# Three 256-column matmuls as one of 256 and one of 512 columns in the one-stream feed-forward products of an exact-float32 network

## The chip, the cores and the metric

The program runs on one core of a Trainium2 chip. The metric is the time of one execution on the device in microseconds (us). Three runs of the kernel before took 2123.69, 2127.23 and 2135.45 us; the median is 2127.23 us.

## What is computed

Two transformer blocks of two layers each, on 256 tokens with 1024 features. Nearly all the arithmetic is matrix products with weights that are read once. Block one has four feed-forward layers around two attention mixers, block two has two mixing sublayers (on two streams of 256 tokens, latent and context) and a feed-forward layer behind each. The feed-forward layers have 2816 hidden features:

```python
def swiglu(x, w1, w3, w2):
    return (jax.nn.silu(x @ w1) * (x @ w3)) @ w2

h = h + 0.5 * swiglu(rmsnorm(h, g[0]), ffn_w1[layer, 0], ffn_w3[layer, 0], ffn_w2[layer, 0])
...
mod = split_cols((sc @ w_mod[l] + b_mod[l])[:, None, :], (D_MODEL,) * N_MOD)
x = layer_norm(ALPHA * x + g1 * y) * ln1_g[l] + ln1_b[l]
x = layer_norm(ALPHA * x + g2 * swiglu_2(modulate(x, sh2, sc2), w_ffn_in[l], w_ffn_out[l])) \
    * ln2_g[l] + ln2_b[l]
```

The context stream goes through layer 0 of block two and is only read as keys and values in layer 1.

## The kernel before

**Exact products.** float32 operands are split into two parts, hi and lo, in a matmul format (`FR`) of the array, with hi + lo equal to the number. A product w x is then three matmuls into one PSUM accumulator, w_hi x_hi, w_hi x_lo and w_lo x_hi; `mm3` (L317) issues them at L323, L324 and L325. The weight block of 128 by 128 is the stationary operand, so each of the three loads weights (rows PEld), and the tokens, 256 columns, stream past it.

**Weights.** All weight blocks are packed in the order of use in one array, in 540 chunks of eight blocks. `Weights.load` brings a chunk in by DMA (tile `wst`), `prepare` makes hi on ACT (L279, `whi`) and lo on VectorE (DVE; L280, `wlo`). Four split chunks are held (`NHL`), so a chunk is split up to four chunks ahead of its use, and a buffer is free when TensorE (PE) has read the chunk in it.

**Up and down.** A feed-forward layer has 22 hidden groups of 128 features. For each group `j` the up loop takes 16 weight blocks (8 over the features, w1 and w3 in turn; two chunks) by `slab_fm`, 48 matmuls into one PSUM bank, 256 columns for w1 and 256 for w3. There are four such banks (tag `mm`). In block one (`ffn1_layer`, L835) the bank is multiplied by 1/rms (L860, DVE, 512 columns, from PSUM to `w`), ACT takes silu of one half (L862), DVE multiplies by the other (L863), and `split` makes the operands of the next product, `ghi` on ACT (L329) and `glo` on DVE (L330). In block two (`up_gen`) silu (L1506) and product (L1507) read the bank itself. The down loop makes eight blocks of 128 output features, each of 22 triples, and adds a block to the residual (L794, L814, L1541).

**One stream and two.** Block one has one stream. In block two, layer 1's feed-forward and parts of layer 0's (six groups each of context and latent, and half of the down products) have one; the rest of layer 0 takes latent and context side by side, with 512 columns per matmul.

**Work beside the loops.** `step` (L332) runs one step of background generators at the end of each group. In three layers of block one `mod_gen` (L691) is one of them: it computes c @ w_mod, 1024 columns at a time, without the array, since it has two vectors only. For each of 16 row blocks it multiplies a loaded `mw` by one column and adds: for the first vector on DVE (L722; the first row block of eight on ACT), for the second on ACT (L725) and GpSimd (POOL; L726). In the second layer `later_gen` builds small tables on DVE as well.

**Order.** Every engine works its queue in order; the queues are laid out by a scheduler from the program's order and its own estimates. Buffers of named pools come free in turn: `w1` has four, `w2` two.

Of the kernel before, what the change touches and what calls it, by code (L numbers as in the profile page):

```python
# [8 lines left out]
FT = mybir.dt.float32  # L9
# [15 lines left out]
# ---------------------------------------------------------------- vector columns  # L25
# [8 lines left out]
# row vectors, broadcast to all partitions: sinks, (g_q, g_k) x2, g_sgu x2  # L34
# [3 lines left out]
# constant columns after the identity: causal, window, cos, sin  # L38
# [85 lines left out]
def _rows(w, groups):  # L124
    """[1024, 1024] by groups of 128-row blocks, each group output-block-major."""
# [4 lines left out]
def _pairs(n, g):  # L130
    """Column order that puts head i of the first group beside head i of the second."""
# [117 lines left out]
# ---------------------------------------------------------------- the kernel  # L249
class Weights:  # L250
    """Streams the packed weights: load, split into two exact float32r parts, hand out blocks."""
# [33 lines left out]
    def block(self, i, w=1):  # L285
        """w adjacent 128-column blocks from block i of the stream."""
# [3 lines left out]
        hi, lo = self.hl[h]  # L290
        c = (i % 8) * 128
        return hi[:, c:c + w * 128], lo[:, c:c + w * 128]
class Body:
# [6 lines left out]
    # ---- small helpers  # L300
# [16 lines left out]
    def mm3(self, ps, w, x, first, last, swap=False):  # L317
# [3 lines left out]
        if swap:  # L321
            (wh, wl), (xh, xl) = (xh, xl), (wh, wl)
# [1675 lines left out]
```

## Time and profile before

| | before |
|---|---|
| median of three runs | 2127.23 us |
| profiled execution, span | 2129.9 us |
| TensorE matmul busy | 2058.5 us, 97% |
| TensorE weight load busy (beside matmuls) | 1885.2 us, 89% |
| VectorE busy | 1509.3 us, 71% |
| ScalarE busy | 1095.1 us, 51% |
| GpSimd busy | 397.0 us, 19% |
| mean granted TensorE clock | 0.983 |

The span is the time from the first to the last instruction of the one execution that the profiler took. A matmul row's length contains its way through the array, so successive rows overlap, and the distance between two starts is what one costs in a stream. VectorE's rows overlap a little in the same way. An engine's busy time says nothing of what it waits for: that is read from the gaps between rows and from what ended them.

### The profile page before, as it was taken

What the parts mean: (1) busy time and instruction counts of PE and PEld (TensorE: products, weight loads), DVE (VectorE), ACT (ScalarE), POOL (GpSimd) and SP (SyncE); (2) the same over time, 40 slices, a digit from 0 to 9 for tenths busy, and PEclk for the clock granted to TensorE, in tenths of its full rate; (3) what the DMA queues carried; (4) which work ended last, traced back from release to release, by engine and by line L of the source; (5) the groups of instructions that cost most, each with busy time, mean ns of one, the idle gap of its engine ahead of it and who ended that gap; (6) DMA issues with size and microseconds to landing.
All of it is one profiled execution on the core that took longest, in us unless ns stands there. A gap on an engine that the chain in (4) does not pass through costs nothing. (4 is left out here: it accounts for less than half of the span.)

```text
span 2129.9 us, 39152 instructions
## 1 busy us (share of the span) xinstructions
PE 2058.5 (97%) x15451; PEld 1885.2 (89%) x15451; DVE 1509.3 (71%) x2646; ACT 1095.1 (51%) x1890; POOL 397.0 (19%) x283
## 2 busy tenths in 40 slices
PE   8999999899999999999999999999999999999997
PEld 8989989889999997999988878888788889779997
DVE  6797886987599566886775867667754468576554
ACT  5564576554566456554544645444432345555443
POOL 1232141321044010210510002213500013003002
PEclk9999999999999999999999988999999999999999
DMA  6775635866576552555541312475663353124553
GB/s 217 266 261 183 199 121 193 268 214 217 179 247 205 190 191 91 197 175 183 185 126 64 107 60 85 141 256 188 203 192 124 130 165 115 52 81 136 181 185 103
DMA packets 117113, 355.40 MB, mean 167 GB/s; under 512 B 21781, under 2 KB 27624, under 8 KB 116480
## 3 DMA queue, kind: packets, MB, share of 16 engines
q1 hardware_dynamic: 115472, 344.54, 49.5%
q10 hardware_dynamic: 1456, 8.36, 1.1%
q8 instruction: 121, 1.98, 0.4%
q14 instruction: 64, 0.52, 0.1%
HBM read 351.66 MB, written 8.90 MB: 169 GB/s over the span
## 5 line engine op out<-in xcount | busy, mean ns | idle before, releaser
L280 DVE TENSOR_TENSOR wlo<-wst,whi 128x1024 fp32r<-128x1024 f32 x540 | 712.1, 1319 | 346.7 <-ACT whi L279 341.2
L323 PE MATMUL mm<-HI,whi 128*128 128x256 f32 (+1 forms) x2944 | 868.6, 297 | 12.9 <-ACT whi L279 8.5
L325 PE MATMUL mm<-HI,wlo 128*128 128x256 f32 (+1 forms) x2944 | 865.6, 295 | 6.7 <-DVE wlo L280 6.7
L324 PE MATMUL mm<-LO,whi 128*128 128x256 f32 (+1 forms) x2944 | 868.5, 296 | 1.1 <-DVE LO L1411 1.1
L279 ACT ACTIVATE whi<-wst 128x1024 fp32r<-128x1024 f32 x540 | 570.0, 1056 | 554.8 <-PE mm L324 307.6
L323 PEld LDWEIGHTS mm<-HI,whi 128*128 128x128 f32 x2944 | 565.4, 193 | 40.5 <-issue 12.5
L324 PEld LDWEIGHTS mm<-LO,whi 128*128 128x128 f32 x2944 | 568.0, 193 | 25.4 <-issue 12.3
L325 PEld LDWEIGHTS mm<-HI,wlo 128*128 128x128 f32 x2944 | 568.0, 193 | 23.6 <-DVE wlo L280 7.8
L325 PE MATMUL mm<-ghi,wlo 128*128 128x256 f32 (+1 forms) x1000 | 288.0, 288 | 2.5 <-DVE wlo L280 2.5
L324 PE MATMUL mm<-glo,whi 128*128 128x256 f32 (+1 forms) x1000 | 287.4, 288 | 1.5 <-DVE glo L330 1.5
L323 PE MATMUL mm<-ghi,whi 128*128 128x256 f32 (+1 forms) x1000 | 286.8, 288 | 0.0
L726 POOL TENSOR_TENSOR macc<-macc,mp 128x1024 f32<-128x1024 f32 (+1 forms) x70 | 168.8, 2411 | 382.0 <-ACT mp L725 346.4
L325 PEld LDWEIGHTS mm<-ghi,wlo 128*128 128x128 f32 x1000 | 191.3, 191 | 8.1 <-issue 3.5
L324 PEld LDWEIGHTS mm<-glo,whi 128*128 128x128 f32 x1000 | 191.4, 191 | 4.4 <-DVE glo L330 2.1
L323 PEld LDWEIGHTS mm<-ghi,whi 128*128 128x128 f32 x1000 | 191.1, 191 | 2.5 <-issue 0.8
L722 DVE SCALAR_TENSOR_TENSOR macc<-mw,sc,macc 128x512 f32<-128x512 f32 (+1 forms) x126 | 161.9, 1285 | 31.7 <-DMA mw<-in_wmod 22.4
L324 PE MATMUL mm<-wlo,HI 128*128 128x256 f32 x352 | 101.2, 288 | 3.4 <-DVE wlo L280 3.4
L323 PE MATMUL mm<-whi,HI 128*128 128x256 f32 x352 | 101.8, 290 | 0.0
L325 PE MATMUL mm<-whi,LO 128*128 128x256 f32 x352 | 100.4, 286 | 0.0
L725 ACT ACTIVATE mp<-mw,sc 128x1024 f32<-128x1024 f32 (+1 forms) x70 | 67.6, 973 | 32.2 <-DMA mw<-in_wmod 24.4
L525 POOL TENSOR_TENSOR sacc<-sacc,w 128x256 f32<-128x256 f32 x36 | 34.5, 959 | 252.7 <-ACT w L521 251.6
L329 ACT ACTIVATE ghi<-w 128x256 fp32r<-128x256 f32 (+1 forms) x120 | 51.1, 426 | 55.0 <-DVE w L863 47.4
(416 smaller groups left out, 2496.9 us busy)
## 6 DMA issues: line engine op xcount, KB each, us to landing
wst<-in_wall SPq DMA_DIRECT2D x540, 512.0 KB
mw<-in_wmod SPq DMA_DIRECT2D x48, 512.0 KB
mw<-in_wmod SPq DMA_DIRECT2D x96, 256.0 KB
brep<-bvec ACTq DMA_DIRECT2D x16, 384.0 KB
nab<-rrep SPq DMA_DIRECT2D x24, 96.0 KB
bias<-brep SPq DMA_DIRECT2D x4, 512.0 KB
bias<-brep SPq DMA_DIRECT2D x8, 256.0 KB
rrep<-in_rpb ACTq DMA_DIRECT2D x4, 348.8 KB
```

Source lines behind the costliest of these rows:

```text
L279: self.marks.append(self.nc.scalar.activation(hi, src, AF.Copy))
L280: self.nc.vector.tensor_tensor(lo, src, hi.bitcast(FT), op=OP.subtract)
L323: nc.tensor.matmul(ps, wh, xh, start=first, stop=False, skip_group_check=True)
L324: nc.tensor.matmul(ps, wh, xl, start=False, stop=False, skip_group_check=True)
L325: nc.tensor.matmul(ps, wl, xh, start=False, stop=last, skip_group_check=True)
L329: self.marks = [self.nc.scalar.activation(hi, src, AF.Copy), self.nc.vector.tensor_tensor(lo, src, hi.bitcast(FT), op=OP.subtract)]
L525: nc.gpsimd.tensor_tensor(st["acc"], st["acc"], sq, op=OP.add)
L722: nc.vector.scalar_tensor_tensor(acc[:, i], w, s, acc[:, i], op0=OP.mult, op1=OP.add)
L725: nc.scalar.activation(t, w, AF.Copy, scale=s)
L726: nc.gpsimd.tensor_tensor(acc[:, i], acc[:, i], t, op=OP.add)
```

## The change

For a product with one stream, hi and lo of x are kept side by side in one tile (`HL`, `ghl`), and mm3 gets a whole bank: w_lo x_hi goes as 256 columns into its first half, then w_hi [x_hi | x_lo] as 512 columns into both. The first half then holds w_lo x_hi + w_hi x_hi and the second w_hi x_lo. The halves are added on the way out: in an up loop by `joined`, where ACT copies the second half to SBUF and DVE adds the first to it; in a down loop by two additions to the residual. An up group takes two banks. The multiplication by 1/rms reads the joined result from SBUF. Hi and lo of a weight chunk lie in one tile (`whl`). Products with two streams, the projections and the attention keep their three matmuls.

```diff
     def prepare(self):
...
-        hi = self.split.tile([128, 1024], FR, name="whi")
-        lo = self.split.tile([128, 1024], FR, name="wlo")
-        self.marks.append(self.nc.scalar.activation(hi, src, AF.Copy))
-        self.nc.vector.tensor_tensor(lo, src, hi.bitcast(FT), op=OP.subtract)
-        self.hl[i] = (hi, lo)
+        w = self.split.tile([128, 2, 1024], FR, name="whl")
+        self.marks.append(self.nc.scalar.activation(w[:, 0], src, AF.Copy))
+        self.nc.vector.tensor_tensor(w[:, 1], src, w[:, 0].bitcast(FT), op=OP.subtract)
+        self.hl[i] = w
...
     def mm3(self, ps, w, x, first, last, swap=False):
...
+        wh, wl = w[:2]
+        xh, xl = x[:2]
+        if len(ps.shape) == 2 and len(xh.shape) == 2 and ps.shape[1] == 2 * xh.shape[1]:
+            nc.tensor.matmul(ps[:, :S], wl, xh, start=first, stop=False, skip_group_check=True)
+            nc.tensor.matmul(ps.rearrange("p (h t) -> p h t", h=2), wh, x[2], start=False, stop=last,
+                             skip_group_check=True)
+            return
         nc.tensor.matmul(ps, wh, xh, start=first, stop=False, skip_group_check=True)
         nc.tensor.matmul(ps, wh, xl, start=False, stop=False, skip_group_check=True)
         nc.tensor.matmul(ps, wl, xh, start=False, stop=last, skip_group_check=True)

+    def joined(self, dst, ps):
+        c = self.w1()
+        self.nc.scalar.activation(c, ps[:, S:], AF.Copy)
+        self.nc.vector.tensor_tensor(dst, ps[:, :S], c, op=OP.add)
...
-        self.HI = self.actp.tile([128, 2, KB, S], FR, name="HI")
-        self.LO = self.actp.tile([128, 2, KB, S], FR, name="LO")
+        self.HL = self.actp.tile([128, 2, KB, 2, S], FR, name="HL")
...
+    def slab_wide(self, x):
+        pss = [self.ps("mm") for _ in range(2)]
+        for k in range(KB):
+            for c in range(2):
+                self.mm3(pss[c], self.W.block(self.wpos + 2 * k + c), self.at(x, k), k == 0, k == KB - 1)
+        self.wpos += 16
+        return pss
...
-                nc.vector.scalar_tensor_tensor(hm, ps, scale, hm, op0=OP.mult, op1=OP.add)
+                for c in (0, S):
+                    nc.vector.scalar_tensor_tensor(hm, ps[:, c:c + S], scale, hm, op0=OP.mult, op1=OP.add)
...
-            gh = gp.tile([128, FB, S], FR, name="ghi")
-            gl = gp.tile([128, FB, S], FR, name="glo")
+            g = gp.tile([128, FB, 2, S], FR, name="ghl")
             for j in range(FB):
-                ps, = self.slab_fm([st["hl"]])
+                pss = self.slab_wide(st["hl"])
...
                 t = self.w2()
-                nc.vector.tensor_tensor(t, ps, st["r"][:, None, :].to_broadcast([128, 2, S]), op=OP.mult)
+                for c in range(2):
+                    self.joined(t[:, c], pss[c])
+                nc.vector.tensor_tensor(t, t, st["r"][:, None, :].to_broadcast([128, 2, S]), op=OP.mult)
...
             for m in range(KB):
-                ps = self.ps("mm")[:, :S]
+                ps = self.ps("mm")
                 for k in range(FB):
-                    self.mm3(ps, self.W.block(self.wpos + k), (gh[:, k], gl[:, k]), k == 0, k == FB - 1)
+                    self.mm3(ps, self.W.block(self.wpos + k), parts(g[:, k]), k == 0, k == FB - 1)
...
     def up_gen(self, js, streams, g, j0):
...
-                ps, = self.slab_fm([self.hl(1 - i)])
+                pss = self.slab_wide(self.hl(1 - i))
+                t = self.w2()
+                for c in range(2):
+                    self.joined(t[:, c], pss[c])
                 sl = self.w1()
-                a, b = ps[:, 0], ps[:, 1]
+                a, b = t[:, 0], t[:, 1]
...
     def down_gen(self, streams, g, evict, nk=FB // 2):
...
+                if len(streams) == 1:
+                    self.mm3(ps, w, parts(g(k, streams[0])), k == 0, k == nk - 1)
+                    continue
```

Two places in the queues show what moves. The first is TensorE's queue in an up loop of block one, before, two blocks of weights:

```order
L323 MATMUL mm<-HI,whi 128x256
L324 MATMUL mm<-LO,whi 128x256
L325 MATMUL mm<-HI,wlo 128x256
L323 MATMUL mm<-HI,whi 128x256
L324 MATMUL mm<-LO,whi 128x256
L325 MATMUL mm<-HI,wlo 128x256
```

and after the change, four blocks of weights of such a loop, the 512-column matmul first or second by where the cut falls:

```order
L332 MATMUL mm<-HL,whl 128x512
L331 MATMUL mm<-HL,whl 128x256
L332 MATMUL mm<-HL,whl 128x512
L331 MATMUL mm<-HL,whl 128x256
L332 MATMUL mm<-HL,whl 128x512
L331 MATMUL mm<-HL,whl 128x256
L332 MATMUL mm<-HL,whl 128x512
```

Three matmuls per block have become two, with the same columns in sum. The second place is VectorE's queue in the third layer's up loop, one group and the start of the next, before (`w` are the buffers of one group, L860 reads the bank, `wlo` are weight splits, L722 is the modulation multiply):

```order
L722 SCALAR_TENSOR_TENSOR macc<-mw,sc,macc 128x1024
L860 TENSOR_TENSOR w_7312<-mm,rstd 128x512
L280 TENSOR_TENSOR wlo<-wst,whi 128x1024
L863 TENSOR_TENSOR w_7314<-w_7314,w_7312 128x256
L280 TENSOR_TENSOR wlo<-wst,whi 128x1024
L330 TENSOR_TENSOR glo<-w_7314,ghi 128x256
L722 SCALAR_TENSOR_TENSOR macc<-mw,sc,macc 128x1024
```

and after the change (L343 is the addition in `joined`, L895 the multiply by 1/rms, L279 the weight split, L898 the product, L353 the low part of the next operand, L754 the modulation multiply):

```order
L754 SCALAR_TENSOR_TENSOR macc<-mw,sc,macc 128x1024
L279 TENSOR_TENSOR whl<-wst,whl 128x1024
L898 TENSOR_TENSOR w_6195<-w_6195,w_6187 128x256
L343 TENSOR_TENSOR w_6250<-mm,w_6251 128x256
L343 TENSOR_TENSOR w_6250<-mm,w_6254 128x256
L279 TENSOR_TENSOR whl<-wst,whl 128x1024
L353 TENSOR_TENSOR ghl<-w_6195,ghl 128x256
L754 SCALAR_TENSOR_TENSOR macc<-mw,sc,macc 128x1024
L895 TENSOR_TENSOR w_6250<-w_6250,rstd 128x512
L279 TENSOR_TENSOR whl<-wst,whl 128x1024
L898 TENSOR_TENSOR w_6258<-w_6258,w_6250 128x256
```

Between two L754 stand two additions more, and the additions of a group come ahead of the low part of the group before. ACT's queue at the same place, after the change (L897 silu, L342 the copies in `joined`, L278 the high part of the weights, L352 of the operand, L757 the second vector's multiply):

```order
L897 ACTIVATE w_6195<-w_6187 128x256
L342 ACTIVATE w_6251<-mm 128x256
L342 ACTIVATE w_6254<-mm 128x256
L278 ACTIVATE whl<-wst 128x1024
L352 ACTIVATE ghl<-w_6195 128x256
L757 ACTIVATE mp<-mw,sc 128x1024
L278 ACTIVATE whl<-wst 128x1024
```

The two copies stand between one group's silu and its high part; before, only a weight split stood there.

## Rows read from the trace of the kernel before

**Rows 1.** The page's busy times: us, share of the span, instructions.

```profile
PE 2058.5 (97%) x15451; PEld 1885.2 (89%) x15451; DVE 1509.3 (71%) x2646; ACT 1095.1 (51%) x1890; POOL 397.0 (19%) x283
```

**Rows 2.** All waits: who waited for whom, us in total, times, longest.

```profile
ACT whi L279 <- PE mm L324: 307.6, 183, 4.5
```

**Rows 3.** Timeline of PE, one stream: start us, us, engine, line, operation.

```profile
1979.75 0.28 PE L323 MATMUL mm<-HI,whi 128*128 128x256 f32 x1
...
1983.95 0.28 PE L325 MATMUL mm<-HI,wlo 128*128 128x256 f32 x1
```

**Rows 4.** Timeline of PE, two streams side by side.

```profile
1649.81 0.39 PE L323 MATMUL mm<-HI,whi 128*128 128x512 f32 x1
...
1654.80 0.39 PE L324 MATMUL mm<-LO,whi 128*128 128x512 f32 x1
```

**Rows 5.** Busy us in four up loops: window, length, PE, PEld, DVE, ACT, POOL.

```profile
83.00:158.00 75.00, 69.83 (x552) 67.13 (x551) 70.53 (x69) 43.65 (x58) 30.16 (x11) 0.98 0.79 267
...
362.00:507.00 145.00, 131.67 (x1035) 126.53 (x1034) 124.93 (x171) 76.84 (x104) 36.40 (x14) 0.95 0.72 238
...
575.00:705.00 130.00, 126.47 (x1029) 122.10 (x1028) 117.66 (x126) 78.36 (x106) 44.49 (x14) 1.00 0.67 218
...
1935.00:2058.00 123.00, 123.00 (x1028) 123.00 (x1027) 68.11 (x88) 58.76 (x89) 0.00 (x0) 1.00 0.57 188
```

**Rows 6.** Timeline of DVE, one step in the third layer's up loop.

```profile
603.98 1.27 DVE L722 SCALAR_TENSOR_TENSOR macc<-mw,sc,macc 128x1024 f32<-128x1024 f32 x1
605.18 0.68 DVE L860 TENSOR_TENSOR w<-mm,rstd 128x512 f32<-128x512 f32 x1
605.78 2.83 DVE L280 TENSOR_TENSOR wlo<-wst,whi 128x1024 fp32r<-128x1024 f32 x1
608.54 0.41 DVE L863 TENSOR_TENSOR w<-w,w 128x256 f32<-128x256 f32 x1
608.87 1.21 DVE L280 TENSOR_TENSOR wlo<-wst,whi 128x1024 fp32r<-128x1024 f32 x1
610.01 0.41 DVE L330 TENSOR_TENSOR glo<-w,ghi 128x256 fp32r<-128x256 f32 x1
610.34 1.27 DVE L722 SCALAR_TENSOR_TENSOR macc<-mw,sc,macc 128x1024 f32<-128x1024 f32 x1
```

**Rows 7.** Timeline of POOL, the same step.

```profile
604.22 3.31 POOL L726 TENSOR_TENSOR macc<-macc,mp 128x1024 f32<-128x1024 f32 x1 [3.06 <-ACT mp L725]
```

**Rows 8.** Timeline of DVE, one step in the first layer's up loop.

```profile
104.30 0.68 DVE L860 TENSOR_TENSOR w<-mm,rstd 128x512 f32<-128x512 f32 x1
...
105.23 3.43 DVE L722 SCALAR_TENSOR_TENSOR macc<-mw,sc,macc 128x1024 f32<-128x1024 f32 x1
...
111.19 0.68 DVE L860 TENSOR_TENSOR w<-mm,rstd 128x512 f32<-128x512 f32 x1
```

**Rows 9.** Timeline of DVE, end of the first layer's up loop.

```profile
155.37 0.68 DVE L860 TENSOR_TENSOR w<-mm,rstd 128x512 f32<-128x512 f32 x1
...
160.52 4.62 DVE L722 SCALAR_TENSOR_TENSOR macc<-mw,sc,macc 128x1024 f32<-128x1024 f32 x2
...
168.74 3.09 DVE L722 SCALAR_TENSOR_TENSOR macc<-mw,sc,macc 128x1024 f32<-128x1024 f32 x1
```

**Rows 10.** Groups by line and form: count, busy us, mean ns, idle before.

```profile
L279 ACT ACTIVATE whi<-wst 128x1024 fp32r<-128x1024 f32 x540 | 570.0, 1056 | 554.8 <-PE mm L324 307.6 <-issue 155.0 <-DMA wst<-in_wall 54.1
...
L722 DVE SCALAR_TENSOR_TENSOR macc<-mw,sc,macc 128x1024 f32<-128x1024 f32 x42 | 83.1, 1979 | 0.0
...
L1507 DVE TENSOR_TENSOR w<-w,mm 128x256 f32<-128x256 f32 x34 | 14.1, 414 | 0.0
...
L1506 ACT ACTIVATE w<-mm 128x256 f32<-128x256 f32 x34 | 12.4, 366 | 0.0
```

**Rows 11.** Timeline of DVE, two 512-column multiplies in the fourth layer.

```profile
961.98 0.69 DVE L1236 TENSOR_TENSOR ex<-ex,rstd 128x512 f32<-128x512 f32 x1
962.58 0.69 DVE L860 TENSOR_TENSOR w<-mm,rstd 128x512 f32<-128x512 f32 x1
```

More of the change, by code (lines that the diff above doesn't have):

```diff
@@ L676, in out_pairs @@
             for k in range(KB):
-                self.mm3(ps, self.W.block(self.wpos + k), (x[0][:, k], x[1][:, k]), k == 0, k == KB - 1)
+                self.mm3(ps, self.W.block(self.wpos + k), self.at(x, k), k == 0, k == KB - 1)
             self.wpos += KB
@@ L1035, in even_mixer @@
                 for k in range(2):
-                    self.mm3(dst, W.block(base + 4 * k + m), (ch[:, k], cl[:, k]), m != 1 and k == 0, k == 1)
+                    self.mm3(dst, W.block(base + 4 * k + m), self.at(chl, k), m != 1 and k == 0, k == 1)
             self.fm_evict(qidx[:, :2], ps.rearrange("p (c t) -> p c t", c=2), r2)
@@ L1242, in pre_norm_gen @@
         nc = self.nc
[L1243 removed]
+        hi, lo = self.hl(1 - i)[:2]
         mu, r = stat.finish()
@@ L1540, in f @@
                 R = self.R[i]
-                nc.vector.scalar_tensor_tensor(R[:, m], ps, self.mod(l, i, 5, m), R[:, m], op0=OP.mult, op1=OP.add)
+                for c in range(0, ps.shape[1], S):
+                    nc.vector.scalar_tensor_tensor(R[:, m], ps[:, c:c + S], self.mod(l, i, 5, m), R[:, m],
+                                                   op0=OP.mult, op1=OP.add)
                 if feed:
@@ L1549, in ffn2_layer @@
             if l == 1:
-                gh, gl = [lambda k, i, t=gp.tile([128, FB, S], FR, name=n): t[:, k] for n in ("ghi", "glo")]
-                self.weave((self.up_gen(range(FB), [0], gh, gl, 0), FB), (self.rests[0], 11))
-                self.finish(self.down_gen([0], gh, gl, evict(True), FB))
+                t = gp.tile([128, FB, 2, S], FR, name="ghl")
+                g = lambda k, i: t[:, k]
+                self.weave((self.up_gen(range(FB), [0], g, 0), FB), (self.rests[0], 11))
+                self.finish(self.down_gen([0], g, evict(True), FB))
                 self.final_norm(stats[0])
@@ L1556, in ffn2_layer, with g @@
             H = FB // 2
-            def store(n, early):
-                one = gp.tile([128, JSEP, S], FR, name=n + "x")
-                two = gp.tile([128, H - JSEP, 2, S], FR, name=n)
-                def f(k, i):
-                    if k >= JSEP:
-                        return two[:, k - JSEP].rearrange("p i t -> p (i t)") if i is None else two[:, k - JSEP, 1 - i]
-                    return None if i is None else early[k] if i else one[:, k]
-                return f
-            gh, gl = [store(n, e) for n, e in zip(("ghi", "glo"), self.early)]
-            both = [0, 1]
-            self.weave((self.up_gen(range(JSEP), [0], gh, gl, 0), JSEP), (self.rests[0], JSEP))
-            self.finish(self.up_gen(range(JSEP, H), both, gh, gl, 0))
-            self.finish(self.down_gen(both, gh, gl, evict(False)))
-            self.finish(self.up_gen(range(H, FB), both, gh, gl, H))
-            self.finish(self.down_gen([0], gh, gl, evict(True)))
+            one = gp.tile([128, JSEP, 2, S], FR, name="ghlx")
+            two = gp.tile([128, H - JSEP, 2, 2, S], FR, name="ghl")
+            def g(k, i):
+                if k >= JSEP:
+                    x = two[:, k - JSEP]
+                    return x.rearrange("p h i t -> p h (i t)") if i is None else x[:, :, 1 - i]
+                return None if i is None else self.early[k] if i else one[:, k]
+            both = [0, 1]
+            self.weave((self.up_gen(range(JSEP), [0], g, 0), JSEP), (self.rests[0], JSEP))
+            self.finish(self.up_gen(range(JSEP, H), both, g, 0))
+            self.finish(self.down_gen(both, g, evict(False)))
+            self.finish(self.up_gen(range(H, FB), both, g, H))
+            self.finish(self.down_gen([0], g, evict(True)))
             self.drain()
```

80 lines of the change are left out of this document (41 added, 39 removed).

## The prediction

> **What bounds the kernel now.** I read the page's busy times first, then the waits, then TensorE's timeline to get its pace, then the busy times by stage. TensorE is busy for 97% of the 2129.9 us span [rows 1], so the program as a whole is paced by its matmuls, and the reader should see that ACT's long waits are waits for TensorE to give weight buffers back [rows 2]. The pace itself: in an up loop with nothing else going on, 35 starts take 1983.95 - 1979.75 = 4.20 us, 120.0 ns for each 256-column matmul [rows 3]. With two streams side by side, 22 starts take 4.99 us, 226.8 ns for 512 columns [rows 4]. So 256 more columns cost 106.8 ns, and every matmul with its own weight load has about 13.2 ns on top.
>
> The share of 97% is a mean, though. Of the four layers of block one, three run the modulation work (L691 to L726) beside their up loop. By stage, VectorE is busy 70.5 of 75, 124.9 of 145 and 117.7 of 130 us there, against 68.1 of 123 in the last layer of block two [rows 5]. One step of the third layer shows who sets the time: from 603.98 to 610.34 seven VectorE rows stand without a gap, 6.36 us, while the group's 48 matmuls need 48 x 0.120 = 5.76 [rows 6]. In that step a weight split takes 2.83 us where the next one takes 1.21, because GpSimd's add runs from 604.22 for 3.31 us [rows 7]; L860, which reads PSUM, runs through that same add in its normal 0.68. In the first layer it is L722 that is held, 3.43 instead of 1.27, and a step is 111.19 - 104.30 = 6.89 us [rows 8]. So these steps are VectorE's, all others TensorE's.
>
> **The change part by part.** *Matmuls.* Wherever one stream is multiplied (mm3's new branch) three matmuls of 256 columns become one of 256 and one of 512. By the program's order 14,842 matmuls become 11,834: 3,008 triples are rewritten, 122 up groups of 16 (88 in block one, 34 in block two) and 1,056 in down loops. A triple is 3 x 120.0 = 360.0 ns, a pair 120.0 + 226.8 = 346.8, so 13.2 ns a triple and 39.7 us if TensorE paced all of them. The columns are the same; only one weight load with its fixed part goes.
>
> The Trainium skill weighs in here. "TensorE: Matmul & The Clock Gate", section Back-to-back issue gap, gives N/2.4 + 2.5 ns for an isolated matmul, by which a triple would fall only by an estimated 2.5 ns; my rows have 13.2 at both widths, and the measurement decides.
>
> *Way out of an up group.* Each group gains two ACT copies of 256 columns from PSUM (366 ns each, L1506 [rows 10]) and two VectorE adds of 256 columns with one operand in PSUM (414 ns, L1507 [rows 10]). Successive VectorE rows start 0.07 to 0.08 us before the one ahead has ended (608.54 + 0.41 against 608.87 [rows 6]), so an add costs 0.335 and the pair 0.67 us. The multiply by rstd stays at 512 columns but reads SBUF twice; L1236 of that kind takes 0.69 like L860 and 0.60 to the next start [rows 11]: no difference where GpSimd is still. ACT has 43.7 to 78.4 us of work in these loops of 75 to 145 [rows 5], so its 0.58 us per group fits; if it did not, the price would be 0.58 x 122 = 71 us, the upper end.
>
> In a step with L722, VectorE without collision needs two splits at 1.135, L860 0.60, two short rows at 0.335 and L722 at 1.20: 4.74 us. With the adds it is 5.41. GpSimd's collision comes on top: 1.62 in the third layer (2.83 - 1.21), 2.16 in the first (3.43 - 1.27). 5.41 + 2.16 = 7.57 us, and TensorE's new group is 48/3 x 0.3468 = 5.55. So the steps that VectorE set before, it sets by more, and TensorE's saving there buys nothing. L722 appears 42 times [rows 10], three of them behind the first layer's last group [rows 9]: 39 steps. In the second layer small table operations crowd the same loop (171 VectorE instructions against 126 [rows 5]); I count 4 more groups. 43 x 0.67 = +28.8 us.
>
> *A collision that gets longer.* In the third layer L860 shielded 0.54 us of the add (2.16 - 1.62), since with an operand in PSUM it ran beside GpSimd [rows 6, 7]. Its successor reads SBUF alone, and in the new order it, or a split, follows L722 directly. If it is held like the splits, 14 steps lose 0.54: +7.6 us; if not, 0. I take 7.6, since the rows that are held here (L280, L722) read SBUF only. The Trainium skill has the same rule, in "GPSIMD Engine Reference", section 8. Key points: GpSimd shares its SBUF interfaces with VectorE, in contention with instructions that have two SBUF inputs. The trace agrees (2.83 against 1.21 for the split, 0.68 unchanged for L860).
>
> *The rest.* The remaining 79 up groups and 1,056 down triples are TensorE's: (79 x 16 + 1,056) x 13.2 ns = 2,320 x 13.2 = -30.6 us. Down evictions double (one more short row of 0.34 us each, by the starts in [rows 6]), beside 22 pairs of 7.6 us per block: hidden, and +0.34 only at the last of each layer. The first group now needs the low half of its weights first, some tenths of a us. Together +1. With two banks a group the four PSUM banks hold two groups instead of four: TensorE may run one group ahead, not three. Where it sets the pace a bank has 5.55 us to be read, against 0.37 + 0.67 of work behind at most one whi on ACT (1.06, L279 [rows 10]) and one split on VectorE: free. If that cover went, it is the second rival.
>
> Sum: -30.6 + 28.8 + 7.6 + 1 = +6.8, so 2129.9 + 6.8 = 2136.7 on the profiled run's clock, whose span is 2.7 above the median of the timed runs (2127.23). I forecast 2134 us. Between the ends: no added VectorE cost (-30.6) would give 2097; all of ACT's copies exposed as well, +71, 2205.
>
> **Rivals.**
> *A. VectorE's idle takes the adds.* The three loops leave VectorE idle for 4.5, 20.1 and 12.3 us [rows 5], 36.9 in sum, about what I add (36.4). If half of it can be used, the time is 2134 - 18 = 2116; if all, 2098. For it: the second layer's 20 us. Against it: the steps of rows 6 have no idle at all, and what is idle lies in steps without L722.
> *B. The new handoff stalls a full queue; slower than before.* In the new order the adds of group j stand in VectorE's queue ahead of the split and glo of the group before, and each waits for an ACT copy that stands behind silu and, at worst, whi (1.06). Behind the waiting add stand wlo, glo, L722 and all that needs them: ghi's partner, GpSimd's add, TensorE's weights. Each of the 43 steps could lose up to 1.06 us: 2134 + 43 x 0.5 = 2156 at half, 2180 at worst. It decides if VectorE idles over 0.25 us per step ahead of the adds. Against it: TensorE, needing 5.55 of 7.57 us, has each group ready some 2 us early.
> *C. The saving does not come.* No row shows a 256- and a 512-column matmul in turn; if the pair keeps the fixed 13.2 ns of the third load, the 30.6 us are gone: 2165, and 2149 if half of it stays. Against it: the 13.2 stands on both widths alike. By the 2.5 ns of the Trainium skill's "TensorE: Matmul & The Clock Gate", Back-to-back issue gap, it would be an estimated 2159.
> *D. Nothing happens* because mm3's branch isn't taken: excluded by TensorE's queue after the change, where 3,008 of the 512-column form stand.
>
> **How the numbers follow.** About 0.5% is what a measurement of this kernel can tell from no change, so 2117 to 2138 counts as the same. Forecast 0.52, own range 2118 to 2148: same 0.41, slower 0.11. A 0.18: faster 0.15, same 0.03. B 0.26: slower 0.24, same 0.02. C 0.04: slower. Together faster 0.15, same 0.46, slower 0.39. The range for 8 in 10 cuts the far halves of A and B: 2110 to 2164.
>
> **What would show it.** Pairs starting every 0.347 us in up loops of the last layer, whose step falls from 5.76 to 5.55. Steps with the modulation multiply at 7.0 to 7.6 us, VectorE full, TensorE waiting on wlo or on banks; the multiply by rstd held to over 2 us beside GpSimd in the third layer. TensorE's busy share falls in the three loops and its clock may dip below 1.00 more often than the 0.95 and 0.98 of rows 5; if it stays low for whole loops, all is slower than my range. If steps stay near 6.4 us, A was right; if VectorE idles ahead of its adds, B.

## The result, and the profile after

The change made the kernel slower: 2188.91 us median of 4 runs (2177.30 to 2190.33) against 2125.46 (2116.03 to 2135.45), a ratio of 1.0292 with a 95% interval of 1.0260 to 1.0324, some 63 us. The forecast was 2134, within a range that ended at 2164: a loss of 7 us became one of 63. The profiled run took 2190.33 us with a span of 2188.5, 58.6 above the profiled span of before.

The page's busy line of the changed kernel, as [rows 1]:

```profile
PE 2060.7 (94%) x12443; PEld 1739.5 (79%) x12443; DVE 1637.7 (75%) x2946; ACT 1168.1 (53%) x2134; POOL 386.8 (18%) x283
```

TensorE starts fewer matmuls, is busy for as long as in [rows 1], and so for a smaller share of a longer program. What it waits for is new. From the waits of the changed kernel (who waits for whom, us in total, times, longest):

```profile
PE mm L331 <- DVE w L343: 59.0, 35, 3.6
DVE w L343 <- ACT w L342: 19.7, 32, 3.5
```

L331 is the first matmul of a pair; it waits for the add L343, that is, for the two banks of the up group two before its own. Among the longer waits of before there was none of the kind.

Where the 58.6 us arise is read by stage. An up loop is measured from the first to the last start of its multiply by rstd (L860, now L895; in block two from product to product), 22 groups each:

| stage, us | before | after | difference | forecast |
|---|---|---|---|---|
| first three up loops | 129.9 + 143.5 + 128.0 | 146.3 + 150.9 + 147.5 | +43.3 | +31.5 |
| fourth up loop | 117.7 | 130.8 | +13.1 | -4.6 |
| block two, first product to first two-stream product | 100.9 | 107.1 | +6.2 | -2.5 |
| last up loop | 118.4 | 115.2 | -3.2 | -4.6 |
| all else (down loops, mixers, ends) | | | -0.8 | -13.0 |
| sum | | | +58.6 | +6.8 |

Each stage is read from one execution of a kernel. The first three up loops, which the runs e1, e10 and e11 below leave as before, took 399.8, 399.7 and 392.9 us there and 401.4 us in the kernel before, so a few us of a stage can't be told from nothing.

The same stretches as busy times, as in [rows 5] (window, length, PE, PEld, DVE, ACT, POOL, granted clock, DMA share, GB/s); they are the up loops of the first, second, third and fourth layer and of the last layer of block two:

```profile
25.00:172.00 147.00, 130.81 (x717) 108.99 (x716) 129.12 (x162) 86.84 (x143) 29.46 (x11) 0.99 0.71 236
381.00:532.00 151.00, 129.92 (x683) 108.84 (x682) 139.10 (x213) 89.57 (x146) 36.61 (x14) 0.92 0.68 224
600.00:748.00 148.00, 129.93 (x695) 109.24 (x695) 138.61 (x163) 89.04 (x148) 37.69 (x14) 0.94 0.60 193
908.00:1040.00 132.00, 122.08 (x671) 104.56 (x670) 106.61 (x182) 78.88 (x148) 15.23 (x14) 0.97 0.52 167
1998.00:2114.00 116.00, 115.27 (x654) 99.84 (x653) 86.50 (x127) 72.11 (x131) 12.10 (x7) 1.00 0.59 190
```

Three cases stand here. In the third layer VectorE is nearly full (138.6 of 148). In the last row nothing is full but TensorE, and the loop got shorter. The fourth row is neither: VectorE has 25 us to spare, and yet TensorE stands still for 10 us and its clock is at 0.97.

**A step of the third layer.** VectorE, from one product to the next, then GpSimd's row (start, us, engine, line), to set beside [rows 6, 7]:

```profile
643.25 0.41 DVE L898 TENSOR_TENSOR w<-w,w 128x256 f32<-128x256 f32 x1
643.59 0.74 DVE L343 TENSOR_TENSOR w<-mm,w 128x256 f32<-128x256 f32 x2
644.25 1.21 DVE L279 TENSOR_TENSOR whl<-wst,whl 128x1024 fp32r<-128x1024 f32 x1
645.38 0.68 DVE L895 TENSOR_TENSOR w<-w,rstd 128x512 f32<-128x512 f32 x1
645.99 2.62 DVE L353 TENSOR_TENSOR ghl<-w,ghl 128x256 fp32r<-128x256 f32 x1
648.53 1.27 DVE L754 SCALAR_TENSOR_TENSOR macc<-mw,sc,macc 128x1024 f32<-128x1024 f32 x1
649.73 1.21 DVE L279 TENSOR_TENSOR whl<-wst,whl 128x1024 fp32r<-128x1024 f32 x1
650.86 0.41 DVE L898 TENSOR_TENSOR w<-w,w 128x256 f32<-128x256 f32 x1
```

```profile
645.68 2.65 POOL L758 TENSOR_TENSOR macc<-macc,mp 128x1024 f32<-128x1024 f32 x1 [5.57 <-ACT mp L757]
```

No gap, and 650.86 - 643.25 = 7.61 us, the 7.57 of the forecast. The two adds take 0.66 (643.59 to 644.25). The row that is held beside GpSimd is the low half of the product (L353), 2.62 us in place of 0.41, and not the multiply L895. L895 had started 0.30 us ahead of GpSimd's add (645.38 against 645.68); L353 is the first row that starts behind it. An L895 that started behind such an add, in the first layer, was held in its turn (VectorE's row, then GpSimd's):

```profile
79.82 2.90 DVE L895 TENSOR_TENSOR w<-w,rstd 128x512 f32<-128x512 f32 x1
```

```profile
79.59 2.59 POOL L758 TENSOR_TENSOR macc<-macc,mp 128x1024 f32<-128x1024 f32 x1 [56.92 <-ACT mp L757]
```

In the groups by line and form this row's mean went from 451 ns before (L330) to 845 after, over 110 rows each (count, busy us, mean ns, idle before):

```profile
L330 DVE TENSOR_TENSOR glo<-w,ghi 128x256 fp32r<-128x256 f32 x110 | 49.6, 451 | 0.5 <-ACT ghi L329 0.5
```

```profile
L353 DVE TENSOR_TENSOR ghl<-w,ghl 128x256 fp32r<-128x256 f32 x110 | 92.9, 845 | 5.1 <-ACT ghl L352 4.8
```

**A stop in the fourth layer.** There is no modulation work there, but the entry of the context stream runs in the background (L1476 to L1485, L1224, L1480). ACT's rows, VectorE's and TensorE's around 920 us:

```profile
917.04 1.06 ACT L278 ACTIVATE whl<-wst 128x1024 fp32r<-128x1024 f32 x1 [1.26 <-PE mm L332]
919.92 1.06 ACT L278 ACTIVATE whl<-wst 128x1024 fp32r<-128x1024 f32 x1 [1.82 <-PE mm L332]
920.88 0.37 ACT L1482 ACTIVATE w<-st 128x256 f32<-128x256 f32 x1
922.60 0.42 ACT L1224 ACTIVATE w<-ex 128x256 f32<-128x256 f32 x1 [1.35 <-DVE ex L1485]
922.93 0.64 ACT L342 ACTIVATE w<-mm 128x256 f32<-128x256 f32 x2
```

```profile
921.01 1.23 DVE L279 TENSOR_TENSOR whl<-wst,whl 128x1024 fp32r<-128x1024 f32 x1 [1.65 <-ACT whl L278]
922.15 0.42 DVE L1485 TENSOR_TENSOR ex<-cx,w 128x256 f32<-128x256 f32 x1
923.32 0.76 DVE L343 TENSOR_TENSOR w<-mm,w 128x256 f32<-128x256 f32 x2 [0.75 <-ACT w L342]
```

```profile
919.44 0.40 PE L332 MATMUL mm<-HL,whl 128*128 128x512 f32 x1
919.67 0.59 PE L1480 MATMUL st<-sacc,ones 128*128 128x256 f32 x2
923.89 0.55 PE L331 MATMUL mm<-HL,whl 128*128 128x256 f32 x1 [3.63 <-DVE w L343]
924.24 0.63 PE L332 MATMUL mm<-HL,whl 128*128 128x512 f32 x1
924.67 0.41 PE L331 MATMUL mm<-HL,whl 128*128 128x256 f32 x1
924.88 0.63 PE L332 MATMUL mm<-HL,whl 128*128 128x512 f32 x1
```

Read it from the end. TensorE's fifth group waits until 923.89 for the banks of the third, whose matmuls ended about 914.0. The adds that empty them wait for ACT's copies at 922.93. Those stand in ACT's queue behind a weight split that waits for TensorE (until 919.92, when the fourth group is over), behind L1482, which reads a sum that TensorE makes behind that fourth group, and behind L1224, which waits for VectorE's L1485, itself behind a weight split. So third and fourth group have to be over before the third is read, and with two groups of banks nothing is left for TensorE to do.

The price is more than the wait. After it pairs start every 0.64 us until about 929.1. The granted clock, third column from the end, of the wait, of the eight pairs after it, and of the time behind those:

```profile
919.90:923.80 3.90, 0.37 (x2) 0.00 (x0) 2.04 (x4) 2.29 (x5) 0.00 (x0) 0.83 0.59 163
923.90:929.10 5.20, 5.20 (x16) 4.48 (x17) 2.88 (x7) 1.91 (x5) 1.42 (x2) 0.50 0.22 81
929.40:934.00 4.60, 4.60 (x28) 4.03 (x28) 2.56 (x4) 2.85 (x4) 0.00 (x0) 1.00 0.00 0
```

0.50 is the lower of the two levels, 1.2 GHz, at which a pair's 768 columns take 0.64 us. Eight pairs lose 8 x (0.64 - 0.35) = 2.3 us there, on top of 3.6 us of wait. The busy share hides this part, since a slow TensorE is a busy one.

### The profile page after: what moved, and what is told of

Read it like the earlier page. It is cut to its first block, busy times and chain, and to the rows that moved or that the text cites. A ratio compares the mean times of both kernels' runs of the same rounds, so it can differ in the third digit from the quotient of the medians.

```text
span 2188.5 us, 33896 instructions
## 1 busy us (share of the span) xinstructions
PE 2060.7 (94%) x12443; PEld 1739.5 (79%) x12443; DVE 1637.7 (75%) x2946; ACT 1168.1 (53%) x2134; POOL 386.8 (18%) x283
## 4 chain that ended last, share of the span: by engine, by line
PE 71%; DVE 17%; issue 6%; ACT 4%; DMA 3%; POOL 0%; ACTq 0%; SPq 0%; DVEq 0%; POOLq 0%
PE mm L332 23%; PE mm L331 12%; PE mm L335 8%; PE mm L336 8%; PE mm L337 8%; DVE whl L279 5%; DVE macc L754 3%; PE sc L1635 3%; DVE ghl L353 2%; ACT whl L278 2%; PE half L1676 2%; DMA mw<-in_wmod 1%; DMA wst<-in_wall 1%; DVE w L343 1%; PE tp L1664 1%
## 5 line engine op out<-in xcount | busy, mean ns | idle before, releaser
L279 DVE TENSOR_TENSOR whl<-wst,whl 128x1024 fp32r<-128x1024 f32 x540 | 682.6, 1266 | 269.3 <-ACT whl L278 267.7
L278 ACT ACTIVATE whl<-wst 128x1024 fp32r<-128x1024 f32 x540 | 569.9, 1057 | 476.1 <-PE mm L332 212.2
L332 PE MATMUL mm<-HL,whl 128*128 128x512 f32 x1952 | 709.4, 408 | 3.5 <-DVE HL L1446 3.3
L331 PE MATMUL mm<-HL,whl 128*128 128x256 f32 x1952 | 557.5, 290 | 76.2 <-DVE w L343 57.9
L331 PEld LDWEIGHTS mm<-HL,whl 128*128 128x128 f32 x1952 | 381.9, 196 | 98.3 <-issue 56.2
L332 PEld LDWEIGHTS mm<-HL,whl 128*128 128x128 f32 x1952 | 376.7, 195 | 92.0 <-issue 4.1
L332 PE MATMUL mm<-ghl,whl 128*128 128x512 f32 x960 | 341.1, 399 | 0.9 <-DVE ghl L353 0.9
L335 PE MATMUL mm<-HL,whl 128*128 128x256 f32 (+1 forms) x992 | 309.3, 318 | 5.2 <-DVE qk_t L1699 3.1
L336 PE MATMUL mm<-HL,whl 128*128 128x256 f32 (+1 forms) x992 | 311.2, 315 | 0.0
L337 PE MATMUL mm<-HL,whl 128*128 128x256 f32 (+1 forms) x992 | 310.2, 315 | 0.0
L331 PE MATMUL mm<-ghl,whl 128*128 128x256 f32 x960 | 270.1, 283 | 7.9 <-DVE whl L279 6.8
L332 PEld LDWEIGHTS mm<-ghl,whl 128*128 128x128 f32 x960 | 180.9, 189 | 45.7 <-issue 1.7
L335 PEld LDWEIGHTS mm<-HL,whl 128*128 128x128 f32 x992 | 187.7, 192 | 26.0 <-issue 10.7
L336 PEld LDWEIGHTS mm<-HL,whl 128*128 128x128 f32 x992 | 190.4, 192 | 17.3 <-issue 6.2
L337 PEld LDWEIGHTS mm<-HL,whl 128*128 128x128 f32 x992 | 190.0, 192 | 14.1 <-issue 2.7
L331 PEld LDWEIGHTS mm<-ghl,whl 128*128 128x128 f32 x960 | 182.2, 190 | 10.9 <-DVE whl L279 7.3
L754 DVE SCALAR_TENSOR_TENSOR macc<-mw,sc,macc 128x512 f32<-128x512 f32 (+1 forms) x126 | 164.4, 1305 | 27.4 <-DMA mw<-in_wmod 18.0
L343 DVE TENSOR_TENSOR w<-mm,w 128x256 f32<-128x256 f32 x244 | 92.5, 416 | 20.4 <-ACT w L342 19.7
L336 PE MATMUL mm<-whl,HL 128*128 128x256 f32 x352 | 101.8, 290 | 3.6 <-DVE whl L279 3.6
L353 DVE TENSOR_TENSOR ghl<-w,ghl 128x256 fp32r<-128x256 f32 (+1 forms) x120 | 100.9, 840 | 5.8 <-ACT ghl L352 5.5
L342 ACT ACTIVATE w<-mm 128x256 f32<-128x256 f32 x244 | 82.1, 375 | 38.6 <-PE mm L332 33.9
```

The costliest lines, as they stand in the source:

```text
L278: self.marks.append(self.nc.scalar.activation(w[:, 0], src, AF.Copy))
L279: self.nc.vector.tensor_tensor(w[:, 1], src, w[:, 0].bitcast(FT), op=OP.subtract)
L331: nc.tensor.matmul(ps[:, :S], wl, xh, start=first, stop=False, skip_group_check=True)
L332: nc.tensor.matmul(ps.rearrange("p (h t) -> p h t", h=2), wh, x[2], start=False, stop=last, skip_group_check=True)
L335: nc.tensor.matmul(ps, wh, xh, start=first, stop=False, skip_group_check=True)
L336: nc.tensor.matmul(ps, wh, xl, start=False, stop=False, skip_group_check=True)
```

## The experiments

Three explanations stood against each other: VectorE has too much work (adds); the way from ACT's copy to VectorE's add stalls queues (handoff); two groups of banks in place of four let TensorE run dry (banks).

**e1**, side by side in the down loops alone. Edit, in both up loops (block one's is shown):

```diff
-                pss = self.slab_wide(st["hl"])
+                ps, = self.slab_fm([st["hl"]])
-                for c in range(2):
-                    self.joined(t[:, c], pss[c])
-                nc.vector.tensor_tensor(t, t, st["r"]...
+                nc.vector.tensor_tensor(t, ps, st["r"]...
```

Expected: 

> Only the down loops multiply hi and lo side by side; the up groups are as before (three matmuls of 256 columns into one bank, one multiply by rstd from PSUM). All theories agree here: 1,056 triples x 13.2 ns = 13.9 us less, 32 second evictions of 0.34 us mostly hidden: 2112 us (2107 to 2118), ratio to the kernel before 0.993 to 0.996. If it is not below 2120, the loss of the changed kernel lies partly in its down loops.

Measured: 2124.15 us, ratio 1.0009 (0.9987 to 1.0032). All theories missed: no gain. In its trace the matmuls of the second, third, fourth and last layer's down loops take 61.4, 62.3, 62.8 and 62.4 us against 64.2, 63.5, 63.9 and 63.5 before, so between 1 and 3 us a loop did come. What is left in all is too little to be told from nothing in timed runs.

**e2**, e1 with the up group's two blocks in two half-used banks:

```diff
-                self.mm3(pss[c], self.W.block(...), self.at(x, k), ...)
+                self.mm3(pss[c][:, :S], self.W.block(...), self.at(x, k), ...)
-                    self.joined(t[:, c], pss[c])
-                nc.vector.tensor_tensor(t, t, st["r"]...
+                    nc.vector.tensor_tensor(t[:, c], pss[c][:, :S], st["r"], op=OP.mult)
```

Expected: 

> Down loops wide; up groups with three matmuls of 256 columns as before, but the two 128-column blocks of a group in two banks of which half is used; two multiplies of 256 columns straight from PSUM, no copy on ACT and no add. Against e1 that changes only how many groups the banks hold (two in place of four) and 0.07 us of VectorE a group. Theory 'banks': TensorE can run only one group ahead, so it stops for VectorE in all layers of block one; 20 to 40 us over e1, 2135 to 2150. Theory 'VectorE's adds' and theory 'handoff over ACT': both are absent here, so as e1 plus at most 4 us: 2110 to 2118.

Measured: 2124.89 us, ratio 1.0018 (0.9998 to 1.0038). The theory "banks" by itself falls: half as many groups cost nothing (0.7 us over e1) as long as one VectorE row straight from PSUM empties a bank. TensorE does wait for banks in its trace, 16.0 us in ten waits (L335 for L894), but the whole is no longer for it.

**e3**, the changed kernel without copies and adds:

```diff
-                    self.joined(t[:, c], pss[c])
-                nc.vector.tensor_tensor(t, t, st["r"]...
+                    nc.vector.tensor_tensor(t[:, c], pss[c][:, :S], st["r"], op=OP.mult)
```

Expected: 

> The changed kernel, but its ACT copies and adds are left out: the up groups read only the first half of each bank, so the product with the low part of x is missing from the up loops' results. Matmuls, banks and weights are those of the changed kernel. Theory 'VectorE's adds' and theory 'handoff': the loss is gone and all 39.7 us of matmul time show, 2085 to 2100. Theory 'banks': the stops of TensorE stay in part: 2120 to 2140.

Measured: 2107.84 us, ratio 0.9930 (0.9904 to 0.9956). By the two ratios to the kernel before (1.0292 and 0.9930) that is 77 us below the changed kernel: its whole loss lies in joining the halves. But it is only 15 us under the kernel before, where 39.7 were due, so the saving of a pair is itself smaller than its term (below).

**e4**, the changed kernel with the second bank from another tag:

```diff
-        pss = [self.ps("mm") for _ in range(2)]
+        pss = [self.ps("mm"), self.ps("up")]
-        tag = "sc" if name in ("st", "tp") else name
+        tag = "sc" if name in ("st", "tp", "up") else name
```

Expected: 

> The changed kernel with the second bank of an up group taken from the three banks that the short sums and transposes use (tag sc), so that three groups and not two fit; copies and adds as in the changed kernel. Theory 'banks': TensorE gets a second group of lead, its waits for L343 fall from 59 us to under 20, and 25 to 45 us come back: 2145 to 2165. Theories 'VectorE's adds' and 'handoff': 2180 to 2195, the waits only move to weights.

Measured: 2222.57 us, ratio 1.0475 (1.0445 to 1.0505), slower than the changed kernel. TensorE's waits in its trace:

```profile
PE mm L331 <- DVE whl L279: 48.9, 26, 9.3
PE st L501 <- DVE lnc L498: 19.1, 2, 13.7
PE st L765 <- DVE macc L754: 16.6, 6, 4.5
```

The wait for banks is gone, as "banks" said, and it bought nothing: TensorE waits nearly as long for the next weights, split by the same VectorE, and the short sums (L501, L765) now share banks with the groups. In the fourth layer's loop (129.9 us against 130.8) the longest wait now stands at such a sum, 6.6 us at L1227 for the add L343. The test isn't clean for that reason: what a third group with banks of its own would do is not shown. Neither theory's figure was met.

**e5 and e6** take the join apart. e5 keeps the adds and drops the copies, e6 keeps the copies and drops the adds:

```diff
 e5
-        c = self.w1()
-        self.nc.scalar.activation(c, ps[:, S:], AF.Copy)
-        self.nc.vector.tensor_tensor(dst, ps[:, :S], c, op=OP.add)
+        self.nc.vector.tensor_tensor(dst, ps[:, :S], self.none, op=OP.add)
 e6
+        self.nc.scalar.activation(dst, ps[:, :S], AF.Copy)
```

Expected of e5: 

> The changed kernel with its two VectorE adds a group, but each adds a constant zero tile in SBUF to the first half of its bank; ACT copies nothing and the second halves (the product with the low part of x in the up loops) are never read. VectorE has the work of the changed kernel, the handoff from ACT is gone. Theory 'VectorE's adds': nearly all of the loss over e3 stays, 2165 to 2190. Theory 'handoff': only the saturated steps pay, 43 x 0.67 = 29 us over e3: 2130 to 2145, and the up loop of the fourth layer takes 114 to 118 us as in e3, not 130.8.

Expected of e6: 

> The changed kernel with its two ACT copies a group, but they copy the first half of each bank straight to where the add would have written, and there is no add; the second halves are never read. VectorE's multiply by rstd waits for ACT as the add did; VectorE has none of the new work. Theory 'VectorE's adds': as e3, 2100 to 2115. Theory 'handoff': the stalls of the fourth layer (130.8 us) stay and the loss over e3 is some 40 us or more: 2145 to 2175.

Measured: e5 2165.07 us, ratio 1.0184 (1.0143 to 1.0225); e6 2123.90 us, ratio 0.9991 (0.9971 to 1.0012). By the ratios the adds alone cost 54 us over e3 and the copies alone 13; e6 lies between the two theories. By stage, in us from first to last multiply (in e3, which has two a group, from the first of the first group to the first of the last):

| stage | e3, neither | e6, copies | e5, adds | changed kernel, both |
|---|---|---|---|---|
| first three | 390.8 | 400.6 | 437.5 | 444.7 |
| fourth | 113.8 | 114.5 | 117.6 | 130.8 |
| block two, as above | 102.3 | 103.8 | 109.3 | 107.1 |

In the first three layers it is VectorE's work: the adds alone bring 46.7 of 53.9 us. In block two's stage, too, the loss comes with the adds (7.0 alone, the copies 1.5). In the fourth loop it is neither part: adds alone 3.8, copies alone 0.7, both, one waiting for the other, 17.0. e5's third and fourth loop show VectorE full in one and TensorE without a gap in the other:

```profile
595.00:742.00 147.00, 130.28 (x699) 108.25 (x698) 137.72 (x162) 79.08 (x106) 39.90 (x14) 0.97 0.60 192
902.00:1020.00 118.00, 118.00 (x669) 102.32 (x668) 107.97 (x182) 66.07 (x105) 18.01 (x14) 1.00 0.57 185
```

**e7**, each join by VectorE alone:

```diff
-        c = self.w1()
-        self.nc.scalar.activation(c, ps[:, S:], AF.Copy)
-        self.nc.vector.tensor_tensor(dst, ps[:, :S], c, op=OP.add)
+        self.nc.vector.tensor_reduce(dst, ps.rearrange("p (h t) -> p t h", h=2), AX.X, OP.add)
```

Expected: 

> The changed kernel with each join done by VectorE alone: one sum over the two halves of the bank (256 results from 512 inputs) in place of ACT's copy and VectorE's add; the computation is whole. VectorE has about 2 x 0.3 us more a group than in the changed kernel, ACT 2 x 0.37 less, and no handoff. Theory 'VectorE's adds': slower than the changed kernel by 43 x 0.6 = 26 us and more, 2205 to 2230. Theory 'handoff': the fourth layer's loop falls to 115 to 120 us and the whole is 2140 to 2175.

Measured: 2191.32 us, ratio 1.0312 (1.0267 to 1.0357), the changed kernel's time; neither theory's figure was met. The row takes 682 ns, so 0.27 us more than an add; what the handoff gave back the load took. Its fourth loop is 126.9 us, with VectorE busy for 121.90 of 128: there, too, VectorE is now the bound.

**e8**, the changed kernel with the fourth layer's background work in one piece ahead of the loop:

```diff
-                self.bg.append(self.ctx_init())
+                self.finish(self.ctx_init())
```

Expected: 

> The changed kernel, with the background work of the fourth layer (ctx_init: the entry of the context stream, sums and norms on all engines) done in one piece ahead of that layer's up loop and not in steps behind each group. Read by stage: first to last multiply by rstd of that loop. Theory 'queue' (the longer way out, copy then add, stands behind background instructions in ACT's and VectorE's queues while only two groups of banks exist): 114 to 118 us in place of 130.8. Theory 'way out' (copy and add in series are too long by themselves): 126 to 132. The whole may be slower, since the work now stands bare: 2180 to 2215.

Measured: the loop takes 113.0 us, 17.8 less than in the changed kernel, with copies, adds and banks untouched; 2188.00 us in all (one run), since the work stands bare ahead of the loop. TensorE's waits for banks in the loop (L331 for L343) fall from 8.3 us to 0.6. Theory "queue" holds for this loop: the way out is short enough by itself and fails only behind the background's rows.

```profile
928.00:1042.00 114.00, 113.37 (x643) 99.34 (x643) 97.02 (x165) 73.86 (x132) 0.00 (x0) 0.99 0.53 178
```

**e9 and e12** leave out GpSimd's additions, in the changed kernel and in the one before:

```diff
-                        nc.gpsimd.tensor_tensor(acc[:, i], acc[:, i], t, op=OP.add)
```

Expected of e9: 

> The changed kernel without GpSimd's additions in the modulation work (L758 left out, so the second modulation vector holds its first term only); VectorE's own multiply-adds L754, copies and adds stay. Theory 'collision' (a step of VectorE is 5.41 us of work and 2.2 us of hold): without the hold the step is 5.41, under TensorE's 5.55, and the first three up loops fall from 146.3, 150.9 and 147.5 us to 120 to 130 each: 2105 to 2130 in all. Theory 'handoff and banks': they keep 135 and more, 2150 to 2175.

Expected of e12: 

> The kernel before without GpSimd's additions in the modulation work (L726 left out, so the second modulation vector holds its first term only): the control for e9. Theory 'collision': VectorE's step falls from 6.36 to 6.89 us to 4.74, TensorE sets 5.76, third layer 14 x 0.6 us, first and second some 10 each, two-stream groups a few: 2090 to 2105, so that e9 (2104) and this differ by under 15 us and the hold explains 50 us or more of the change's loss of 63. Theory 'adds, whatever GpSimd does': this comes out at 2060 or less.

Measured: e9 2103.81 us, ratio 0.9899 (0.9874 to 0.9925); e12 2077.40 us, ratio 0.9792 (0.9756 to 0.9828). Without the hold the change costs some 25 us and not 63 (26 between the medians, 23 between the ratios). e9 alone would have told a false story, that the hold is worth 85 us; the kernel before gains 47 by the same edit. Neither theory was right on the size: the third layer behaves as "collision" has it (121.0 against 121.7 us, no loss left), the first and second still lose 12.9 and 8.3.

**e13, e14, e15** remove the hold with the computation whole, VectorE taking over the second multiply-add, in the changed kernel (e13), in the kernel before (e15), and in e11, which is described below (e14):

```diff
-                    elif i == 0:
-                        nc.vector.scalar_tensor_tensor(acc[:, i], w, s, acc[:, i], op0=OP.mult, op1=OP.add)
                     else:
-                        t = pool.tile([128, CW], FT, name="mp", bufs=2)
-                        nc.scalar.activation(t, w, AF.Copy, scale=s)
-                        nc.gpsimd.tensor_tensor(acc[:, i], acc[:, i], t, op=OP.add)
+                        nc.vector.scalar_tensor_tensor(acc[:, i], w, s, acc[:, i], op0=OP.mult, op1=OP.add)
```

Expected of e13: 

> The changed kernel with the second vector's multiply-add done by VectorE as the first one's is (one more instruction of 1.20 us from start to start a step), no scaled copy on ACT and nothing on GpSimd; the computation is whole. Theory 'collision': the step goes from 5.41 + 2.21 = 7.62 to 5.41 + 1.20 = 6.61 us, 39 steps x 1.0 = 39 us less: 2140 to 2160. Theory 'load of VectorE, hold of no account': 1.2 us more a step, 2215 to 2240.

Expected of e15: 

> The kernel before with the second vector's multiply-add on VectorE and nothing else changed. By the same working 16 to 37 us under the kernel before: 2088 to 2108. The difference from e14 is what side by side is worth where VectorE has time for it: 5 to 10 us by e11, nothing by e1.

Expected of e14: 

> e11 (side by side in all down loops and the last up loop, the wide matmul first) with the second vector's multiply-add on VectorE as in e13. The step in the three up loops is 4.74 + 1.20 = 5.94 us in place of 6.36 to 6.89: 16 to 37 us under e11, 2080 to 2102, below the kernel before by 1 to 2%. If the modulation work is late for its readers without GpSimd: 2110 or more.

Measured: e13 2152.13 us, ratio 1.0126 (1.0080 to 1.0173); e15 2087.80, ratio 0.9837 (0.9813 to 0.9860); e14 2082.67, ratio 0.9804 (0.9782 to 0.9827). All three came out as expected, e15 at the lower edge: one row of 1.2 us on VectorE is cheaper than a hold of 2.2. But e13 is 64 us over e15, as much as the changed kernel over the one before, though no hold is left: 42.9 of them in the first three loops, where two adds in 39 steps are 26, 11.9 in the fourth and 6.2 in block two's stage. So the price of the change goes with how full VectorE is: with 1.2 us more of its own work a step it is that of a kernel with the hold, with neither (e9 against e12) some 25. The third loop of each, e13 first, and then e13's in two parts:

```profile
581.00:725.00 144.00, 127.97 (x698) 107.82 (x697) 126.34 (x179) 75.54 (x135) 0.00 (x0) 0.96 0.62 198
```

```profile
548.00:675.00 127.00, 127.00 (x1037) 123.11 (x1037) 108.93 (x132) 62.12 (x88) 0.00 (x0) 1.00 0.69 222
```

```profile
596.30:643.70 47.40, 42.70 (x241) 36.52 (x240) 45.86 (x60) 22.64 (x40) 0.00 (x0) 1.00 0.76 240
643.70:724.70 81.00, 69.67 (x368) 57.63 (x367) 66.56 (x98) 40.27 (x75) 0.00 (x0) 0.94 0.54 172
```

In e15 TensorE has no gap. In e13 VectorE is full in the first part (45.9 of 47.4 us). In the second neither engine is (69.7 and 66.6 of 81), and the clock is at 0.94. There TensorE waits 11.3 us for banks (L331 for L343), and VectorE 12.0 us for ACT's weight splits, which wait for TensorE to give buffers back: they wait for each other in turn.

**e10 and e11** keep side by side where VectorE has time, in the down loops and the last up loop; e11 puts the wide matmul first:

```diff
 e10, up_gen
+                if len(js) == FB:
                     pss = self.slab_wide(self.hl(1 - i))
...
+                else:
+                    ps, = self.slab_fm([self.hl(1 - i)])
 e11, mm3
+            nc.tensor.matmul(ps.rearrange("p (h t) -> p h t", h=2), wh, x[2], start=first, stop=False, ...
+            nc.tensor.matmul(ps[:, :S], wl, xh, start=False, stop=last, ...
```

Expected of e10: 

> Hi and lo side by side only where VectorE has time: in all down loops and in the up loop of the last layer of block two (22 groups), everything else as before. By the pair at 0.347 to 0.353 us: 1,056 x (6.7 to 13.2 ns) + 352 x (6.7 to 13.2 ns) = 9.4 to 18.6 us less, a few us given back by second evictions: 2110 to 2120, ratio 0.994 to 0.998. If the saving of a pair were really nothing: 2125.

Expected of e11: 

> As e10, but of each pair the 512-column matmul goes first and the 256-column one second. It asks what sets the two periods of a pair, 0.347 and 0.353 us, that the traces of e1 and of the changed kernel show from one loop to the next. If the order within the pair decides, one period stands in all loops: at 0.347 everywhere 3 to 5 us below e10, at 0.353 everywhere the same or 3 us above it. If it is chance (how the loop begins), both periods appear as before and the time is that of e10, within 3 us.

Measured: e10 2121.00 us, ratio 0.9991 (0.9972 to 1.0011); e11 2117.48, ratio 0.9972 (0.9952 to 0.9993). e10 shows no gain, e11 a small one; the intervals overlap, so that the order matters isn't shown. Both periods of a pair appear in both kernels (0.3467 and 0.3533 us in e10's second and third down loop, 0.3532 and 0.3534 in e11's, 0.3466 in e11's last): the order doesn't set them.

The best of all is e14, 2.0% under the kernel before. Most of that is e15's, which has nothing of the change; side by side adds 5 us (0.9804 against 0.9837, intervals that overlap, but all four runs of e14, 2078.38 to 2085.54 us, lie under all four of e15, 2087.18 to 2094.13).

## Why the prediction was wrong

*The step that failed* is the rest: "The remaining 79 up groups and 1,056 down triples are TensorE's", with its claim that a bank "has 5.55 us to be read ... free". It gave -30.6 us and came out above zero. The fourth layer's 22 groups were to gain 4.6 us and lost 13.1, and block two's single groups lost 6.2. The time that I set against 5.55 us was that of the rows of the way out and one split on either engine. What counts is what stands ahead of them in two queues that work in order: in the stop at 920 us, 8.9 us of waits and background between the group's end (914.0) and its copies (922.93). I had looked for such a stall (rival B), but only in the 43 steps with modulation work, where its price was 22 us at half; I had excluded it where VectorE has time to spare. e8 shows that the background's rows make it, e5 and e6 that it needs the copy and the add in series. e2 shows that two groups of banks were harmless without them. In block two's stage it is the adds (e5) that the term left out.

*VectorE's adds*: right in kind and in the step (7.57 forecast, 7.61 measured), too small in sum: the first three loops lose 43.3 us where the terms gave 31.5. (The step of rows 6 has six VectorE rows and not seven: the last one shown opens the next step. Its length is right.) The hold is not what was too small. Added up over the adds of 1024 columns in these loops, what VectorE's held rows take beyond their usual length went from an estimated 18.6, 28.2 and 23.6 us in the three layers to 24.1, 25.7 and 30.0: 9.4 us more, where the sum had 7.6. The remaining 10 us are something else. e13 shows turn-taking in the absence of any hold, and 50 pairs of the three loops ran at the lower clock, at some 0.29 us more each, against 15 triples before. How much of that shows in the time beside a nearly full VectorE is open.

*The collision*: the place was wrong. L895 takes 0.68 us in almost every row; L353, with 0.41 us of work, took the hold in its stead. The sum didn't notice, because a full hold costs the same wherever it falls (2.21 us on L353, 2.16 on L722). The Trainium skill's rule ("GPSIMD Engine Reference", 8. Key points) names instructions with two SBUF inputs: L353 is one, and so is L895, so it says which rows can be held, not which will be. In the two cases above it is the first such row that starts behind GpSimd's add.

*The saving of a pair* (13.2 ns): between half and whole. Pairs start every 0.3467 or every 0.3533 us, so 13.3 or 6.7 ns are saved, and the last up loop, paced by TensorE alone, gained 3.2 us where 4.6 was due. Rival C was half right. The 2.5 ns of the Trainium skill's "TensorE: Matmul & The Clock Gate" (Back-to-back issue gap) would give an estimated 0.3575 us for a pair after a triple of 0.360, which no loop shows.

*The clock*: I let it be a remark. In the stop at 920 us the slow pairs add 2.3 us to a wait of 3.6; the granted clock of the second and third loop is 0.92 and 0.94.

Rival A was wrong: VectorE's idle time didn't take the adds. Rival B was right that the handoff stalls full queues, and wrong in the place: in the first three loops VectorE waits 5.6 us in all for a copy ahead of its adds, where B had 22 at half. D was rightly excluded.

## What to carry to other kernels

Shorter work on the engine that sets the pace can be worth less than nothing if it lengthens the way out of its buffers: count what stands ahead of each row of that way in every in-order queue, background work above all, and hold the sum against the number of buffers, not the rows' own durations against a step. An engine that is nearly full beside another that holds it can make an added row cost more than its length; moving the holder's work onto the held engine (e15) can be cheaper than the hold. A control of the kernel before with the same edit (e12 to e9) is what keeps a leave-out from telling a false size.

## What the hardware showed that I had not expected

- A pair of a 256- and a 512-column matmul has two periods, 0.3467 and 0.3533 us, each constant over tens of us of a loop; the same down loop has one in e1 and the other in the changed kernel. What chooses is not found.
- GpSimd's add of 1024 columns holds one VectorE row for up to 2.2 us whatever that row's own length: 0.41 became 2.62 (L353, above), 1.27 became 3.43 (L722, [rows 8]). Where a row with an operand in PSUM ran beside the add first, the next row lost 1.62 (2.83 against 1.21, [rows 6]).
- In the stop at 920 us, a wait of 3.6 us, TensorE's granted clock fell to 0.50 and stayed there for the 5.2 us of the eight pairs behind it. Behind a wait of 2.8 us in the first loop (until 133.56) it was 0.50 as well, from 134.0 to 137.4. At that level a pair takes 768 columns at 1.2 GHz (0.64 us) with no fixed part to be seen.
